# An already tuned two-block kernel whose build orders instructions by its other account of time

## The chip, the cores and the metric

The kernel runs on one core of a Trainium2 chip. The metric is the device time of one execution in microseconds, as the median of several runs. The engines are TensorE (PE in the profile, with PEld its weight loads), VectorE (DVE), ScalarE (ACT), GpSimd (POOL) and the queue that issues most DMAs (SP).

## What is computed

One sequence of 256 tokens with 1024 channels goes through two blocks, all in float32. The first has two layers; each layer is a half-weighted SwiGLU FFN, a mixer stage that feeds three sequence mixers from one projection, and another half FFN. The second block is an attention and convolution mixer modulated by a vector c, and a convolved SwiGLU FFN. The reference, cut:

```python
for l in range(2):
    x = x + 0.5 * swiglu(rms_norm(x, ffn1_norm[l]), ffn1_w_gate_up[l], ffn1_w_down[l])
    u = rms_norm(x, mix_norm[l]) @ w_in[l]
    u_ssd, u_ml, u_rw = jnp.split(u, [D_SSD_IN, D_SSD_IN + D_MLSTM_IN], axis=-1)
    y = concatenate([ssd_mixer(u_ssd, ...), mlstm_mixer(u_ml, ...), rwkv7_mixer(u_rw, ...)])
    x = x + y @ w_out[l]
    x = x + 0.5 * swiglu(rms_norm(x, ffn2_norm[l]), ffn2_w_gate_up[l], ffn2_w_down[l])
x = rms_norm(x, final_norm)
mod = silu(c) @ w_ada + b_ada                     # six vectors: shift, scale, gate, twice
h = rms_norm(x, g_mix) * (1 + sc1) + sh1
q, k, v, u, c_gate, b_gate = split(h @ w_in_2)
conv = b_gate * causal_dwconv(c_gate * u, conv_w, conv_b)
x = x + gt1 * (concat([rms_norm(attention(q, k, v)), rms_norm(conv)]) @ w_out_2)
h = rms_norm(x, g_ffn) * (1 + sc2) + sh2
val, gte = split(causal_dwconv(h @ w_up, ...))
out = rms_norm(x + gt2 * ((silu(gte) * val) @ w_down), g_final)
```

## The kernel before

Activations lie channels-first: a tile is 128 channels by 256 tokens. All weights come in as one stream of 128x128 blocks, seven to a chunk, in the order in which the program asks for them: `fetch` issues the DMA of a chunk (`raw`, L145), ScalarE casts it to a high part (`whi`, L155), VectorE makes the rest (`wlo`, L156). A dense product takes three matmuls for each block, high by high, high by low and low by high (`mm`, L172 to L176; in the profile L92, output `d`, of which there are three PSUM banks). The small float32 matmuls and transposes of the mixers are recorded at L95, output `m`, with four banks, when they belong to a chain that `weave` runs.

The mixer stage (`mixers`, L406) is where different kinds of work mix. The projection w_in is 40 column tiles, computed two at a time in the order of `IN_PAIRS`; each pair (`d_...`) takes 48 matmuls or more, and its results go through ScalarE and VectorE (`conv_silu` L394 to L401, `shifted` L426 to L430, the gates' input `dtg` L457, `sz` L476). Five generators run beside it: rwkv in two halves of four heads, the gates, the SSD heads and the mLSTM heads. `weave` (L508) decides in which order the program emits pairs of w_in, steps of the generators and tiles of w_out.

The steps that matter below, of one rwkv half: the kk norm (L569 to L597, matmuls `m_2814` and `m_2831` in the first layer's first half); the triangular inversion in two levels, for which four copies L699 each assemble `Tm` and `TT` (`w2_3296` and `w2_3297` for half 0, `w2_3948` and `w2_3949` for half 1), L719 and L723 take the products from PSUM, L732 and L733 subtract; then four chunks of state steps, each a ring from TensorE over a copy `R` (L756), a matmul, `uv` (L761), a matmul and the state `S` on VectorE (L771, L774), with the result copied by L780. The gates' block is one chain on ScalarE and VectorE (L824 to L837) with three loads of activation tables. The SSD heads fetch rows of the gates from DRAM (L1066), and ScalarE turns each into decays: four L1078 and one L1079 for each tile.

The program's order is a wish, not the queue. The tile framework collects all instructions, and its list scheduler then writes one in-order queue for each engine from dependencies, from priorities (`tc.high_priority`, in `first` and around the weight casts) and from an account of when each engine would be free. Semaphores are placed afterwards; the pools' buffers and PSUM banks rotate as written.

## Time and profile before

| | |
|---|---|
| median of 3 runs | 1607.62 us (1605.43 to 1609.72) |
| profiled execution | 1615.12 us, span 1613.3 us |
| mean granted TensorE clock in it | 0.986 of full |
| busy share: TensorE, its weight loads, VectorE, ScalarE | 97%, 94%, 72%, 61% |
| weights read | 287.5 MB, 179 GB/s over the span |

All stage times below are those of the one profiled execution: FFN 1 of layer 0 until about 208 us, its mixers until 485, FFN 2 until 668, FFN 1 of layer 1 until 850, its mixers until 1122, FFN 2 until 1300, the attention stage until 1415, the last FFN until 1613. Busy TensorE time counts from an instruction's start to its end while matmuls overlap, so what a dense matmul costs is read from how far apart their starts lie.

### The profile page before, as it was taken

The numbers are of one execution on the slowest core, as the hardware profiler recorded it, in microseconds if no ns is written. First come the engines' busy times: TensorE is split into PE (matmuls) and PEld (weight loads), VectorE is DVE, ScalarE is ACT, GpSimd is POOL, SyncE is SP. The second block draws the span as 40 slices with busy tenths as digits, with TensorE's granted clock in tenths as the row PEclk, the third lists the DMA queues.
The fourth block names the chain that finished last, engine by engine and source line by source line (L and its number), as shares of the span: only waits on it lengthen the run. The fifth ranks groups of instructions, "written<-read, shape, count | busy, mean of one in ns | idle before, by whom it ended". The sixth has DMA issues, their size and how long they took to land.

```text
span 1613.3 us, 33769 instructions
## 1 busy us (share of the span) xinstructions
PE 1561.7 (97%) x13660; PEld 1509.1 (94%) x13660; DVE 1161.1 (72%) x1965; ACT 990.7 (61%) x1684; POOL 44.6 (3%) x66
## 2 busy tenths in 40 slices
PE   8999998999999999999999999999999999999998
PEld 7999988879999999999998887899999998999997
DVE  7765689757777655787568975778785676698863
ACT  6554587878655444555457777866555565587753
POOL 0000001000000000000000100000000000000000
PEclk9999999899999999999999989999999999999999
DMA  7866644334357666597664333446886653456662
GB/s 255 296 205 190 200 127 127 96 117 140 115 174 258 222 184 194 185 336 253 192 197 134 119 100 113 140 126 202 296 310 189 190 159 115 149 163 189 188 193 73
DMA packets 106717, 290.81 MB, mean 180 GB/s; under 512 B 15640, under 2 KB 28096, under 8 KB 106432
## 3 DMA queue, kind: packets, MB, share of 16 engines
q1 hardware_dynamic: 106272, 288.12, 56.4%
q8 instruction: 107, 1.75, 0.5%
q10 hardware_dynamic: 288, 0.52, 0.1%
q14 instruction: 50, 0.41, 0.1%
HBM read 287.51 MB, written 1.09 MB: 179 GB/s over the span
## 4 chain that ended last, share of the span: by engine, by line
PE 71%; issue 16%; DVE 6%; ACT 5%; POOL 1%; DMA 0%; DVEq 0%; POOLq 0%; SPq 0%; ACTq 0%
PE d L92 60%; PE m L95 8%; PE m L92 3%; DVE wlo L156 1%; ACT whi L155 1%; PE st L92 1%; POOL stm L233 1%; ACT w L699 1%; DVE am L628 0%; DVE pair L227 0%; DVE tmp L338 0%; DVE w L399 0%; DVE pair L399 0%; ACT w L426 0%; DMA x<-xT 0%
## 5 line engine op out<-in xcount | busy, mean ns | idle before, releaser
L92 PE MATMUL d<-pair,whi 128*128 128x256 f32 x5344 | 960.3, 282 | 4.8 <-ACT whi L155 2.2
L92 PEld LDWEIGHTS d<-pair,whi 128*128 128x128 f32 x5344 | 824.3, 190 | 17.0 <-issue 6.3
L156 DVE TENSOR_TENSOR wlo<-raw,whi 128x896 fp32r<-128x896 f32 x544 | 590.9, 1089 | 250.5 <-ACT whi L155 247.2
L92 PE MATMUL d<-pair,wlo 128*128 128x256 f32 x2672 | 755.7, 283 | 3.9 <-DVE wlo L156 3.9
L155 ACT CAST whi<-raw 128x896 fp32r<-128x896 f32 x544 | 511.3, 943 | 329.0 <-PE d L92 232.8
L92 PEld LDWEIGHTS d<-pair,wlo 128*128 128x128 f32 x2672 | 509.2, 191 | 9.2 <-DVE wlo L156 5.2
L92 PE MATMUL d<-hp,whi 128*128 128x256 f32 x1760 | 302.7, 277 | 0.0
L92 PEld LDWEIGHTS d<-hp,whi 128*128 128x128 f32 x1760 | 265.9, 188 | 0.0
L92 PE MATMUL d<-hp,wlo 128*128 128x256 f32 x880 | 243.4, 277 | 0.0
L92 PEld LDWEIGHTS d<-hp,wlo 128*128 128x128 f32 x880 | 165.5, 188 | 0.0
L226 ACT CAST hp<-h 128x256 fp32r<-128x256 f32 x88 | 35.4, 406 | 93.3 <-DVE h L366 93.2
L95 PE MATMUL m<-w,w 64*64 64x64 f32 (+5 forms) x848 | 66.9, 260 | 8.1 <-issue 4.3
L95 PEld LDWEIGHTS m<-w,w 64*64 64x64 f32 (+3 forms) x848 | 55.6, 155 | 15.3 <-issue 11.9
L1146 DVE SCALAR_TENSOR_TENSOR adasum<-ada,sc,adasum 128x1024 f32<-128x1024 f32 x42 | 53.8, 1281 | 17.6 <-DMA ada<-ada 17.6
L227 DVE TENSOR_TENSOR hp<-h,hp 128x256 fp32r<-128x256 f32 x88 | 36.8, 422 | 15.3 <-ACT hp L226 14.5
L92 PE MATMUL d<-w,whi 128*128 128x256 f32 x256 | 45.6, 281 | 0.0
L1179 DVE SCALAR_TENSOR_TENSOR up<-raw,par,up 128x255 f32<-128x255 f32 (+1 forms) x88 | 37.2, 479 | 10.6 <-ACT raw L1175 10.4
L365 ACT ACTIVATE s<-d 128x256 f32<-128x256 f32 x80 | 30.4, 380 | 22.7 <-PE d L92 21.8
L95 PE MATMUL m<-cst,w 128*128 128x128 f32 (+1 forms) x166 | 29.6, 297 | 11.0 <-DVE w L989 4.1
L95 PE MATMUL m<-w,am 64*64 64x64 f32 (+1 forms) x512 | 33.7, 230 | 6.7 <-issue 6.7
L95 PEld LDWEIGHTS m<-w,am 64*64 64x64 f32 (+1 forms) x512 | 27.4, 140 | 13.4 <-issue 9.2
L92 PEld LDWEIGHTS d<-w,whi 128*128 128x128 f32 x256 | 39.1, 189 | 0.0
(341 smaller groups left out, 1481.2 us busy)
## 6 DMA issues: line engine op xcount, KB each, us to landing
raw<-ws SPq DMA_DIRECT2D x544, 448.0 KB, 3.9
ada<-ada SPq DMA_DIRECT2D x48, 512.0 KB, 6.4
w<-da SPq DMA_DIRECT2D x16, 256.0 KB, 4.9
w<-small SPq DMA_DIRECT2D x10, 256.0 KB, 4.4
ab<-abias SPq DMA_DIRECT2D x1, 1536.0 KB, 7.9
x<-xT SPq DMA_DIRECT2D x4, 256.0 KB, 5.5
w<-da SPq DMA_DIRECT2D x8, 128.0 KB, 3.4
w<-dw SPq DMA_DIRECT2D x4, 256.0 KB, 5.0
```

The costliest lines, as they stand in the source:

```text
L92: return op(*args, **kw)
L95: return op(*args, **kw)
L155: S.copy(hi, raw)
L156: V.tensor_sub(lo, raw, hi.bitcast(F32))
L226: S.copy(hi, src)
L227: V.tensor_sub(lo, src, hi.bitcast(F32))
L233: G.tensor_tensor(dst, m, mhalf.to_broadcast([128, n]), op=OP.pow)
L365: S.activation(s, p[:, 0], AF.Silu)
L699: S.copy(dst[g, :, o:o + 32].rearrange("p s (b c) -> p s b c", b=2), et[g, :, :, 0:8].rearrange("p c b s -> p s b c"))
L1146: V.scalar_tensor_tensor(acc, w, sc[:, k:k + 1], acc, op0=OP.mult, op1=OP.add)
L1179: V.scalar_tensor_tensor(dst[:, i, d:], raw[:, i, :T - d], P(w, 3 * j + k), dst[:, i, d:], op0=OP.mult, op1=OP.add)
```

## The change

The context that holds the list scheduler gets one argument. With it the scheduler takes its other account of time, a timeline for each engine, when it decides which ready instruction comes next. No instruction is added or taken away, the weight stream keeps its order, and GpSimd's queue is the same; the queues of TensorE, VectorE, ScalarE and SP are written in other orders.

```diff
     order = []
-    with tile.TileContext(nc) as tc:
+    with tile.TileContext(nc, schedule_with_timeline_sim=True) as tc:
         _program(tc, aps, order)
     r = run_bass_kernel_spmd(nc, [_pack(inp, order)], core_ids=[0])
```

Three places in the mixers of layer 0; layer 1 repeats each.

ScalarE around the first half's inversion. Names: `w2_3296` and `w2_3297` are Tm and TT, `w2_3531` the gates' input, `w2_3565` and `w2_3566` the gates' block. Before:

```order
L699 COPY w2_3296<-w2_3043 32x8x32 x4
L695 ACTIVATE w2_3042<-w2_3044,cst_71 128x16x16 x2
L719 ACTIVATE w2_3428<-m_3430,cst_71 128x8x16 x2
L699 COPY w2_3297<-w2_3043 32x8x32 x4
L457 ACTIVATE w2_3531<-d_3494,par_70 128x256
L155 CAST whi_3761<-raw_3626 128x896
L824 ACTIVATE w2_3565<-w2_3531 64x256
L394 ACTIVATE pair1_3252<-d_3721,par_70 128x256
L825 ACT_TABLE_LOAD
L825 ACTIVATE w2_3565<-w2_3565 64x256
```

Now:

```order
L824 ACTIVATE w2_3565<-w2_3531 64x256
L825 ACT_TABLE_LOAD
L825 ACTIVATE w2_3565<-w2_3565 64x256
L155 CAST whi_3870<-raw_3738 128x896
L827 ACT_TABLE_LOAD
L827 ACTIVATE w2_3566<-w2_3565 64x256
L395 COPY w2_3637<-d_3576 128x512
L695 ACTIVATE w2_3042<-w2_3044,cst_71 128x16x16 x2
L830 ACT_TABLE_LOAD
L830 ACTIVATE w2_3565<-w2_3566 64x256
L155 CAST whi_3897<-raw_3765 128x896
L699 COPY w2_3296<-w2_3043 32x8x32 x4
```

The gates' block with its three table loads stood behind both groups of L699; now the whole of it stands ahead of the first group, and a fourth load (L401) stands ahead of the second. Ahead of these rows now come two L394 that read d_3721. On TensorE `m_3430`, which reads Tm, stood behind 31 matmuls of d_3721; now it stands behind all 48 of d_3863 and 18 of d_4019, and 30 more of d_4019 follow it.

TensorE at the second half's inversion and its first state steps (`m_4280` second level, `m_4306`, `m_4313`, `m_4416`, `m_4433` the steps of chunks 0 and 1; `m_4398` to `m_4400` the first half's output; `m_4442` the SSD heads). Before:

```order
L95 MATMUL m_4280<-w2_3949,w2_4186 64x64
L95 MATMUL m_4306<-w2_3682,am_3395 64x64 x2
L92 MATMUL d_4471<-pair0_2490,whi_4251 128x256 x2
L92 MATMUL d_4471<-pair0_2490,wlo_4252 128x256
L92 MATMUL d_4471<-pair0_2490,whi_4345 128x256 x2
L92 MATMUL d_4471<-pair0_2490,wlo_4346 128x256
```

Now:

```order
L95 MATMUL m_4280<-w2_3949,w2_4186 64x64
L95 MATMUL m_4306<-w2_3682,am_3395 64x64
L95 MATMUL m_4280<-w2_3949,w2_4186 64x64
L95 MATMUL m_4306<-w2_3682,am_3395 64x64 x2
L95 MATMUL m_4313<-R_4311,w2_3949 64x64 x4
L95 MATMUL m_4306<-w2_3682,am_3395 64x64 x4
L95 MATMUL m_4398<-cst_71,w2_3706 128x128
L95 MATMUL m_4399<-cst_71,w2_3162 128x128
```

Before, ten matmuls of d_4471 stood between these rows of m_4306 and m_4313, and more between the later steps; now the steps follow each other. From m_4280 to m_4919, the last SSD group, there were 158 dense matmuls and are now 48, all of d_5014. The dense tiles d_4471 to d_4856 stand ahead of m_4188, the first matmul group of that level. Earlier in the stage, 15 dense matmuls stood between m_2814 and m_2831 and 46 do now.

ScalarE from the copy `R_4311`, which m_4313 reads, to L780, which empties the bank of m_4306 (`w2_4321` to `w2_4326` are the SSD heads' decays). Before, from that copy on:

```order
L756 COPY R_4311<-m_4306 64x256
L155 CAST whi_4502<-raw_4376 128x896
L761 ACTIVATE w2_3682<-m_4313 64x256
L1078 ACTIVATE w2_4321<-w2_4321,nat_3842 128x128 x4
L1078 ACTIVATE w2_4322<-w2_4322,nat_3842 128x128
L1079 ACTIVATE w2_4321<-w2_4321 128x512
L806 ACTIVATE w2_4411<-m_4398,par_70 128x256
L780 COPY w2_4305<-m_4306 64x256
L1078 ACTIVATE w2_4322<-w2_4322,nat_3842 128x128
L806 ACTIVATE w2_4411<-m_4398,par_70 128x256
L1078 ACTIVATE w2_4322<-w2_4322,nat_3842 128x128 x2
L155 CAST whi_4529<-raw_4479 128x896
```

Now, from the row behind that copy on:

```order
L1078 ACTIVATE w2_4321<-w2_4321,nat_3842 128x128 x4
L1078 ACTIVATE w2_4322<-w2_4322,nat_3842 128x128
L761 ACTIVATE w2_3682<-m_4313 64x256
L1078 ACTIVATE w2_4322<-w2_4322,nat_3842 128x128 x3
L1079 ACT_TABLE_LOAD
L1079 ACTIVATE w2_4321<-w2_4321 128x512
L1078 ACTIVATE w2_4325<-w2_4325,nat_3842 128x128 x4
L1078 ACTIVATE w2_4326<-w2_4326,nat_3842 128x128 x4
L1079 ACTIVATE w2_4322<-w2_4322 128x512
L1079 ACTIVATE w2_4325<-w2_4325 128x512
L806 ACTIVATE w2_4411<-m_4398,par_70 128x256
L780 COPY w2_4305<-m_4306 64x256
```

Between the copy and L780 stood five L1078 and one L1079; now 16 L1078, a table load and three L1079 do.

## Rows read from the trace of the kernel before

**Rows 1.** The page, busy time: engine, us busy, share of the span.
```profile
PE 1561.7 (97%) x13660; PEld 1509.1 (94%) x13660; DVE 1161.1 (72%) x1965; ACT 990.7 (61%) x1684; POOL 44.6 (3%) x66
```

**Rows 2.** Chain of work that ended last: start us, us, what.
```profile
30.49 93.91 PE d L92 x826
```

**Rows 3.** Windows: us, busy PE, PEld, DVE, ACT, POOL, clock, DMA share, GB/s.
```profile
208.00:485.00 277.00, 260.70 (x2396) 242.93 (x2394) 214.13 (x433) 202.96 (x372) 16.89 (x21) 0.97 0.42 128
485.00:668.00 183.00, 182.49 (x1577) 181.87 (x1578) 119.09 (x159) 93.08 (x139) 0.82 (x2) 1.00 0.66 208
```

**Rows 4.** Timeline, TensorE: start us, us, what, [idle before <- releaser].
```profile
226.43 1.05 PE L95 MATMUL m<-cst,w 128*128 128x2 f32 x8 [1.15 <-ACT w L575]
...
230.11 0.66 PE L95 MATMUL m<-cst,w 128*128 128x128 f32 x4 [0.75 <-ACT w L586]
...
240.29 1.16 PE L95 MATMUL m<-w,w 64*128 64x128 f32 x16 [0.71 <-DVE w L617]
...
252.86 1.33 PE L95 MATMUL m<-cst,w 128*128 128x2 f32 x10 [1.06 <-ACT w L575]
```

**Rows 5.** Timeline, TensorE, at cluster A.
```profile
275.56 0.38 PE L92 MATMUL d<-pair,wlo 128*128 128x256 f32 x1 [1.15 <-DVE wlo L156]
...
282.00 1.15 PE L95 MATMUL m<-w,am 64*64 64x64 f32 x32 [1.85 <-issue]
...
295.84 1.03 PE L95 MATMUL m<-w,w 64*64 64x64 f32 x28 [2.17 <-issue]
```

**Rows 6.** Timeline, ScalarE, the gates' block.
```profile
286.42 0.47 ACT L457 ACTIVATE w<-d,par 128x256 f32<-128x256 f32 x1
286.79 0.93 ACT L155 CAST whi<-raw 128x896 fp32r<-128x896 f32 x1
...
287.94 0.55 ACT L394 ACTIVATE pair<-d,par 128x256 f32<-128x256 f32 x1
288.51 1.28 ACT L825 ACT_TABLE_LOAD   x1
289.80 0.42 ACT L825 ACTIVATE w<-w 64x256 f32<-64x256 f32 x1
...
294.18 0.42 ACT L830 ACTIVATE w<-w 64x256 f32<-64x256 f32 x1
```

**Rows 7.** Timeline, TensorE, at cluster B.
```profile
336.43 0.76 PE L95 MATMUL m<-w,am 64*64 64x64 f32 x19 [1.50 <-issue]
...
340.55 0.65 PE L95 MATMUL m<-w,w 64*64 64x64 f32 x15 [0.73 <-ACT w L719]
...
354.89 0.30 PE L95 MATMUL m<-cst,w 128*128 128x128 f32 x1 [0.52 <-DVE w L794]
```

**Rows 8.** Windows over one stretch: all instructions, then those of L95 alone.
```profile
349.60:393.09 43.49, 42.97 (x407) 38.07 (x406) 28.72 (x53) 34.84 (x77) 1.64 (x1) 1.00 0.40 122
...
349.60:393.09 43.49, 23.84 (x248) 19.23 (x248) 1.00 0.40 122
```

**Rows 9.** Groups by line, ScalarE, 208 to 485: busy us, mean ns, idle before.
```profile
L1078 ACT ACTIVATE w<-w,nat 128x128 f32<-128x128 f32 x32 | 10.3, 392 | 0.0
L699 ACT COPY w<-w 32x256 f32<-32x256 f32 x16 | 10.2, 636 | 0.1
...
L1079 ACT ACTIVATE w<-w 128x512 f32<-128x512 f32 x8 | 4.9, 622 | 0.0
...
L780 ACT COPY w<-m 64x256 f32<-64x256 f32 x8 | 2.9, 365 | 4.4 <-PE m L95 4.4
```

**Rows 10.** Windows as in rows 3, of two short stretches.
```profile
283.70:287.10 3.40, 3.40 (x25) 3.17 (x25) 2.75 (x7) 3.34 (x7) 0.00 (x0) 0.50 0.78 217
297.30:307.60 10.30, 10.30 (x55) 8.81 (x54) 5.46 (x14) 5.65 (x12) 0.53 (x1) 0.50 0.16 46
```

**Rows 11.** Timeline, TensorE, end of the mixers.
```profile
405.78 0.43 PE L95 MATMUL st<-cst,stm 128*128 128x128 f32 x2 [0.57 <-POOL stm L233]
...
433.76 1.01 PE L95 MATMUL m<-cst,w 128*128 128x128 f32 x4 [1.91 <-DVE w L989]
```

## The prediction

> **What bounds the kernel now.** I read the page's busy times first: TensorE is busy for 97% of the span [rows 1], so whatever another order gives or takes must come out of TensorE's idle time and of how fast it runs. Next I read the chain of work that ended last: its long pieces are dense matmuls of one kind, 826 in 93.91 us, 113.7 ns each [rows 2]. That is the price of a dense matmul as cover: ten of them hide 1.1 us. The table of windows by stage then says where idle time is at all. An FFN stage has 182.49 us of TensorE work in 183 us; a mixer stage has 260.70 in 277 [rows 3] (the mixers of layer 1 read 257.62 in 272, the same pattern). So the mixers are the place: 16 us of idle in each, and beside it some 10 us in which TensorE runs at the half clock level. TensorE's timeline over the mixers gives the waits one by one. They fall into four clusters: early, where the first rwkv half starts [rows 4]; cluster A, its triangular inversion [rows 5]; cluster B, the second half's inversion and state steps [rows 7]; and the end [rows 11].
>
> **The change part by part.** No instruction is added or removed, so every term is a wait that moves. All cover is dense w_in matmuls: 16 tiles' worth, used up sooner or later.
>
> *Early: a gain.* Before, waits of 1.15, 0.75, 0.71 and 1.06 us, 3.67 in sum [rows 4]. Now more dense work stands ahead of each: between the kk norm's two steps m_2814 and m_2831 46 dense matmuls instead of 15, 31 × 0.1137 = 3.5 us more cover than the 0.75 us wait needs. I leave 0.3 us: **−3.4 us** per mixers. If the cover came too late for all of them the gain would be 0.
>
> *Cluster A: a loss.* Before, TensorE waits 1.15 + 1.85 + 2.17 = 5.17 us [rows 5]. In the old order the copies L699, which level 0 of the inversion needs, run ahead of the gates' block on ScalarE (L457 to L830 with its three table loads). In the new order that block stands ahead of them. From before's trace the block lasts from 286.42 to 294.60, 8.2 us [rows 6]; in the new order it holds two L695 (128x256 like L394) in place of two L394. Count from the end of d_3721, which the first row L394 ×2 reads:
> ScalarE: two L394 1.0, the block 8.2, a weight cast 0.93, four L699 2.5 (0.636 each [rows 9]), less 0.1 at each of three joins (neighbours overlap by about that: L155 starts at 286.79, before L457's 0.47 us from 286.42 are over): 12.3 us until m_3430 may start. TensorE meanwhile: d_3863 needs the bank that L457 empties, a wait of 1.6 us; then 48 + 18 dense matmuls, 7.5 us. So m_3430 waits 12.3 − 9.1 = 3.2 us. Then ScalarE has two L695 (1.2, each as an L1079), a cast (0.93), two L394 (1.0), a fourth table load (1.28 [rows 6]) with its L401 (0.62, as an L1079), four L699 (2.5) and two L719 (0.6, smaller than an L780 each), less overlaps 7.5 us, against m_3430 and 30 dense matmuls, 1.15 + 3.4 = 4.6 us: 2.9 us. Sum 7.7 against 5.17: **+2.5 us** per mixers. If the casts and L695 run in gaps it is 0; I keep +5 as the upper end.
>
> The sum takes a table load at 1.28 us with nothing around it: L825's load starts at 288.51 and its activation at 289.80 [rows 6]. The Trainium skill, page "ScalarE: Activation LUTs", section "What ACT_TABLE_LOAD costs", counts about 1.38 us of drain on top of each load, 2.66 us a switch. No such drain shows in that row; by that rule the four loads in this chain would add an estimated 5.5 us per mixers, 11 us in all, and the time would come to about 1632 us.
>
> *Cluster B: the main loss.* In the stretch 349.60 to 393.09 TensorE is idle for 0.5 us only, because 158 dense matmuls stand between the rwkv steps; the L95 matmuls are 248 of its 407 records [rows 8]. In the new order 48 remain there (d_5014): 110 × 0.1137 = 12.5 us of cover was spent earlier. TensorE's own work left is 43.0 − 12.5 = 30.5 us, and ScalarE's in-order queue between L723 and the last L1079 (68 instructions and three loads, at the means of [rows 6, 9] by shape 35.1 us, less 0.1 per join) 29 us: two queues of equal length that hand work back and forth, so each handover now shows. The largest, from the end of the copy R_4311: m_4313 waits for that copy (0.5 us: 0.37 [rows 9] and the two handovers); the next m_4306 waits for L761 behind five L1078 (five in 1.6 us, and 0.38: 1.5 us after TensorE is ready); and m_4416, which takes the bank that L780 empties, waits until ScalarE has done 16 L1078 (6.27), a table load (1.28), three L1079 (1.87), L761 (0.38, shaped as L780), one L806 (0.55, as an L394 [rows 6]) and L780, 10.7 us less 22 joins of 0.1 = 8.5 us, while TensorE, from 2.0 on, has 20 matmul records ahead of it at 0.1 us (24.9 us of L95 work over 248 in [rows 8]) and the fill of two short groups, until about 4.5: 4.0 us. Sum so far 6.0. Behind it stand the state copy and the steps m_4433, m_4465, m_4550, later m_4587, m_4692, m_4711 and m_4919 with nothing or one short group between them; at half a us each seven such steps make 3.5 us, of which I take 3 as some overlap. Together 9 us, against 1.50 + 0.73 + 0.52 = 2.75 before [rows 7]: **+6.2 us** per mixers. Bounds: with all handovers hidden −2.75, with every step at 0.7 us and the bank wait repeated once +11.
>
> *End and stage starts: nothing.* Before, 0.57 and 1.91 us at the end [rows 11]. Now w_out starts before the last rwkv group and waits for it; I put that at the same 2.5 us, from 0 to 5. At the other stage starts waits of 0.5 to 1.5 us come and go in both directions (a tile's h is made ahead of part of the activations' low half in some, behind it in others): 0, from −4 to +4 in all.
>
> *The clock.* TensorE's granted clock is 0.50, the 1.2 GHz level, from 283.70 to 287.10 and from 297.30 to 307.60 [rows 10]; ahead of them lie the waits that end at 282.00 and 295.84 [rows 5]. Cluster B's new waits are longer than those, so I count one more such stretch of 10.3 us per mixers. If dense work filled it, half its length, 5 us, would be lost; about 40% of it is dense or back to back work: **+2 us** per mixers (0 to 5).
>
> **Sum.** Per mixers −3.4 + 2.5 + 6.2 + 2 = +7.3, two layers +14.6, rounded to +14: against the profiled execution's 1615.1 us that is 1629, and against the median, 7.5 us below that execution, **1621 us**.
>
> **Rivals.**
> *Faster, the handovers stay hidden.* ScalarE's exponentials L1078/L1079 need only the gates and a load, no rwkv result. If ScalarE reaches them while TensorE still works off dense tiles, cluster B costs its floor, −2.75. Then a mixers costs −3.4 + 2.5 − 2.75 and no clock term, −3.7; with −2 at stage starts 1598 us. For it: ScalarE is busy only 202.96 of 277 us [rows 3], so it has slack to run ahead. Against: L723 behind m_4188 stands ahead of all those L1078 in its queue, and the dense tiles are used up before m_4188. It decides once cluster B's waits fall below 3.6 us.
> *No change.* Waits only change place: A +2.5, B +1, early −3.4, so 1607 us within 0.3% (5 us, about what a measurement of this kernel can tell from no change). For it: ScalarE and TensorE have the same work in B. Against: the 4.0 us bank wait alone exceeds that.
> *Much slower, the tail at half clock.* If TensorE is held at 1.2 GHz through the whole tail of each mixers, its 30.5 us of work there grows by up to 15; as part of that lies under waits, +10: per mixers +15, 1638 us. For it: 10.3 us at 0.50 followed two waits of 1.85 and 2.17 us [rows 5, 10]. Against: the 48 dense matmuls of d_5014 lie in between.
>
> **How the numbers follow.** My forecast, slower by 5 to 22 us, gets 0.48; much slower 0.12; the drain rule 0.03; no change 0.15; faster 0.22. Slower is then 0.63. The range 1597 to 1641 reaches to the faster rival's time and to the much slower one's; the forecast's own range is 1612 to 1631.
>
> **What would show it.** Right: early waits at L575 and L586 gone; in both mixers waits before m_3430 and at level 0's second group of 2 to 4 us, released by L699 and L719; a stretch some 30 us long near the end of w_in in which L95 rows follow each other with waits on L756, L761, L774 and L780, 8 us or more in sum. FFN stages as long as before within 2 us. Wrong: a mixers not longer than 277 us; the tail's L1078 done before m_4306; or a difference that sits in the FFN stages, say by weight casts that come late.

## The result, and the profile after

The changed kernel takes **1665.38 us** (median of 4 runs, 1663.71 to 1667.92) where the kernel before took 1606.71 beside it: 1.0355 times as long, 95% interval 1.0334 to 1.0376. The forecast was 1621, the range ended at 1641. The direction was right; the size was a quarter of what came (+14 forecast, +58.7 measured). The profiled executions lie 52.8 us apart, since that of the kernel before was some 8 us above its median.

The page of the changed kernel, busy times: TensorE's work is what it was, its share is not.

```profile
PE 1573.8 (94%) x13660; PEld 1525.2 (92%) x13660; DVE 1161.9 (70%) x1965; ACT 989.1 (59%) x1684; POOL 45.0 (3%) x66
```

Against [rows 1] the busy time grew by 12 us and the span by 52.8, so 40.7 us are new idle time of TensorE. The next two views are windows by stage, columns as in rows 3, with the stages cut at TensorE's last matmul of a named tile (`d_2517`, `d_5823`, `d_8136`, `d_10499`, `d_13809`, `d_16048`, `d_17279`), so that both kernels are cut at the same work. The order of the rows is FFN 1, mixers, FFN 2 of layer 0, the same of layer 1, attention, last FFN. Before:

```profile
0.00:209.30 209.30, 202.65 (x1714) 198.11 (x1715) 139.70 (x203) 111.21 (x170) 3.03 (x12) 1.00 0.70 225
209.30:479.10 269.80, 254.52 (x2344) 236.94 (x2343) 208.42 (x425) 199.12 (x366) 16.89 (x21) 0.97 0.43 128
479.10:666.40 187.30, 185.78 (x1607) 184.96 (x1606) 121.90 (x164) 95.48 (x143) 0.82 (x2) 1.00 0.66 207
666.40:851.10 184.70, 183.62 (x1616) 182.10 (x1615) 130.21 (x180) 95.61 (x144) 1.06 (x4) 1.00 0.72 236
851.10:1119.70 268.60, 254.22 (x2343) 236.71 (x2343) 208.39 (x426) 198.81 (x367) 16.93 (x21) 0.97 0.44 135
1119.70:1291.10 171.40, 171.22 (x1510) 169.81 (x1510) 122.52 (x161) 91.01 (x139) 0.00 (x0) 1.00 0.73 239
1291.10:1409.60 118.50, 114.90 (x899) 107.71 (x898) 80.74 (x156) 68.59 (x136) 4.24 (x4) 0.97 0.45 140
1409.60:1613.30 203.70, 194.76 (x1644) 192.74 (x1642) 149.24 (x255) 130.88 (x224) 1.60 (x2) 0.99 0.53 162
```

After:

```profile
0.00:212.20 212.20, 205.49 (x1715) 201.65 (x1715) 136.99 (x197) 110.45 (x168) 2.06 (x12) 0.99 0.69 224
212.20:492.60 280.40, 253.20 (x2342) 237.06 (x2341) 208.99 (x421) 197.76 (x364) 18.02 (x21) 0.95 0.40 122
492.60:683.60 191.00, 187.02 (x1608) 185.98 (x1606) 122.12 (x168) 96.25 (x144) 0.82 (x2) 0.99 0.64 205
683.60:871.30 187.70, 185.97 (x1616) 184.35 (x1615) 129.99 (x179) 95.99 (x145) 0.88 (x4) 1.00 0.70 234
871.30:1155.50 284.20, 255.65 (x2342) 239.91 (x2341) 209.08 (x422) 197.85 (x365) 18.63 (x21) 0.95 0.40 125
1155.50:1334.10 178.60, 174.62 (x1512) 173.10 (x1511) 125.04 (x170) 93.02 (x143) 0.00 (x0) 0.99 0.70 230
1334.10:1460.90 126.80, 117.67 (x899) 109.96 (x898) 80.66 (x157) 69.35 (x137) 3.20 (x4) 0.92 0.42 130
1460.90:1666.10 205.20, 194.14 (x1644) 193.16 (x1642) 149.00 (x255) 128.42 (x222) 1.39 (x2) 0.98 0.53 161
```

Length less busy TensorE is a stage's idle time. The two mixers are 10.6 and 15.6 us longer, and their idle time grew by 11.9 and 14.2. The six other stages, for which the forecast had nothing, are 26.6 us longer: 14.6 of it is idle time, and 12.0 is the same work running longer beside a lower granted clock (attention from 0.97 to 0.92; the clock's missing share times the length, summed over the six stages, grew from 5.6 to 20.1 us).

Where in the mixers: windows of layer 0 cut at the first matmul of `m_2814`, `m_3430` and `m_4188`. The last row is the tail. Before:

```profile
209.30:226.40 17.10, 15.93 (x134) 14.96 (x132) 13.20 (x21) 15.23 (x25) 0.00 (x0) 1.00 0.52 152
226.40:282.00 55.60, 49.20 (x438) 46.50 (x439) 52.04 (x119) 40.60 (x69) 7.74 (x10) 1.00 0.39 121
282.00:346.40 64.40, 59.76 (x638) 53.92 (x638) 45.05 (x106) 51.87 (x88) 2.42 (x5) 0.89 0.39 113
346.40:479.10 132.70, 129.63 (x1136) 121.57 (x1135) 98.13 (x182) 91.41 (x185) 6.74 (x6) 0.99 0.44 136
```

After:

```profile
212.20:229.30 17.10, 16.90 (x144) 16.19 (x143) 15.03 (x26) 15.88 (x27) 0.00 (x0) 1.00 0.43 136
229.30:295.60 66.30, 58.14 (x513) 55.67 (x511) 63.25 (x147) 50.59 (x84) 8.87 (x10) 1.00 0.42 133
295.60:364.30 68.70, 65.47 (x732) 60.77 (x732) 44.10 (x88) 49.62 (x83) 2.41 (x5) 0.98 0.42 123
364.30:492.60 128.30, 112.69 (x957) 104.43 (x956) 86.60 (x164) 81.67 (x172) 6.74 (x6) 0.91 0.38 113
```

Idle time changed by -1.0, +1.8, -1.4 and, in the tail, +12.5 us (layer 1, cut alike: -1.1, +3.4, +0.3 and +11.5). So the tail makes the loss. Its waits, from TensorE's timeline after:

```profile
369.83 0.35 PE L95 MATMUL m<-R,w 64*64 64x64 f32 x3 [2.10 <-DVE lst L790]
...
374.12 1.11 PE L95 MATMUL m<-w,am 128*64 128x64 f32 x8 [3.65 <-ACT w L761]
...
381.29 0.87 PE L95 MATMUL m<-w,w 128*128 128x128 f32 x4 [2.66 <-ACT w L780]
...
406.28 0.68 PE L95 MATMUL m<-S,w 128*128 128x128 f32 x4 [0.91 <-DVE S L774]
...
420.28 0.50 PE L92 MATMUL d<-w,whi 128*128 128x256 f32 x2 [1.60 <-ACT w L395]
...
426.27 2.93 PE L95 MATMUL m<-w,w 128*128 128x256 f32 x16 [1.06 <-ACT w L401]
```

With seven smaller ones that are left out here, ten waits in cluster B make 12.4 us and three at the end 3.2, where [rows 7, 11] had 2.75 and 2.5. (One more, 1.70 us at 338.19 behind L761, stands ahead of `m_4188` and is not among the ten.) ScalarE's timeline beside the second wait shows why it is 3.65:

```profile
372.10 1.57 ACT L1078 ACTIVATE w<-w,nat 128x128 f32<-128x128 f32 x5 [2.73 <-DMA w<-da]
373.69 0.38 ACT L761 ACTIVATE w<-m 64x256 f32<-64x256 f32 x1
```

L761, which `m_4306` waits for, stands behind five L1078, as the forecast had it; but those five first wait 2.73 us themselves, for rows of the gates from DRAM (L1066). Layer 1 does not repeat this place: there L761 stands ahead of the L1078 in ScalarE's queue (1034.01 against 1035.89), and the waits of its counterparts of `m_4313`, `m_4306` and `m_4416` read:

```profile
1033.04 0.65 PE L95 MATMUL m<-R,w 64*64 64x64 f32 x8 [0.72 <-DVE w L733]
1034.44 0.68 PE L95 MATMUL m<-w,am 128*64 128x64 f32 x8 [0.76 <-ACT w L761]
...
1044.54 1.22 PE L95 MATMUL m<-w,w 128*128 128x128 f32 x4 [4.16 <-ACT w L780]
```

The start of an FFN, which the forecast passed over: TensorE at FFN 2 of layer 0, the last statistics matmul and the next two waits.

```profile
492.59 0.38 PE L92 MATMUL st<-cst,stm 128*128 128x128 f32 x2
495.92 0.38 PE L92 MATMUL d<-pair,whi 128*128 128x256 f32 x1 [2.95 <-ACT pair L226]
497.32 0.39 PE L92 MATMUL d<-pair,whi 128*128 128x256 f32 x1 [1.02 <-DVE pair L227]
```

The first tiles of an FFN (`d_5822`, `d_5823`) read activations that are not normalized yet and need no statistics; the next (`d_5968`) wait for `rb`, L226 and L227. Before, 54 matmuls of `d_5822` and `d_5823` stood behind the statistics matmul and ran while that chain ended, 54 x 0.1137 = 6.1 us of cover; now none does, all stand ahead of it. Before, that place read:

```profile
472.71 0.38 PE L92 MATMUL st<-cst,stm 128*128 128x128 f32 x2
472.85 0.48 PE L92 MATMUL d<-pair,whi 128*128 128x256 f32 x2
```

### The profile page after: what moved, and what is told of

Read it like the earlier page. It is cut to its first block, busy times and chain, and to the rows that moved or that the text cites. A ratio compares the mean times of both kernels' runs of the same rounds, so it can differ in the third digit from the quotient of the medians.

```text
span 1666.1 us, 33832 instructions
## 1 busy us (share of the span) xinstructions
PE 1573.8 (94%) x13660; PEld 1525.2 (92%) x13660; DVE 1161.9 (70%) x1965; ACT 989.1 (59%) x1684; POOL 45.0 (3%) x66
## 4 chain that ended last, share of the span: by engine, by line
PE 60%; issue 12%; DVE 5%; ACT 5%; DMA 1%; POOL 0%; POOLq 0%; DVEq 0%; SPq 0%; ACTq 0%
PE d L92 51%; PE m L95 6%; PE m L92 3%; DVE wlo L156 1%; DMA w<-da 1%; ACT w L1078 1%; PE st L92 1%; ACT whi L155 1%; DVE tmp L338 0%; ACT w L699 0%; ACT L401 0%; DVE am L628 0%; DVE w L641 0%; ACT w L1079 0%; ACT L1079 0%
## 5 line engine op out<-in xcount | busy, mean ns | idle before, releaser
L155 ACT CAST whi<-raw 128x896 fp32r<-128x896 f32 x544 | 512.3, 944 | 447.0 <-PE d L92 307.8
L92 PE MATMUL d<-hp,whi 128*128 128x256 f32 x1760 | 306.1, 279 | 0.1
L95 PE MATMUL m<-w,w 64*64 64x64 f32 (+5 forms) x848 | 74.2, 275 | 15.4 <-ACT w L780 6.8
L95 PEld LDWEIGHTS m<-w,w 64*64 64x64 f32 (+3 forms) x848 | 61.7, 164 | 25.7 <-ACT w L780 8.0
L226 ACT CAST hp<-h 128x256 fp32r<-128x256 f32 x88 | 35.0, 403 | 30.3 <-DVE h L366 30.2
L95 PE MATMUL m<-w,am 64*64 64x64 f32 (+1 forms) x512 | 34.2, 235 | 14.2 <-issue 7.7
L95 PEld LDWEIGHTS m<-w,am 64*64 64x64 f32 (+1 forms) x512 | 28.2, 145 | 20.7 <-issue 10.2
L366 DVE TENSOR_TENSOR h<-s,d 128x256 f32<-128x256 f32 x88 | 36.1, 415 | 5.2 <-ACT s L365 5.2
L227 DVE TENSOR_TENSOR hp<-h,hp 128x256 fp32r<-128x256 f32 x88 | 36.3, 418 | 1.9 <-ACT hp L226 1.9
```

Source lines behind the costliest of these rows:

```text
L92: return op(*args, **kw)
L95: return op(*args, **kw)
L155: S.copy(hi, raw)
L226: S.copy(hi, src)
L227: V.tensor_sub(lo, src, hi.bitcast(F32))
L366: V.tensor_mul(h, s, p[:, 1])
```

## The experiments

Two theories stood at first. Theory C, cover: the new account spends dense matmuls early, and the slow chains end with nothing beside them. Theory S, queue: the state loads L1066 stand behind weight chunks on SP, and ScalarE waits for them. Later runs set the orders of engines, not of single instructions, against each other. A kernel's stage times come from its one profiled execution.

**State loads on another queue (e1, e4).** In the changed kernel, and as a control in the one before:

```diff
-                    nc.sync.dma_start(t, da[q * 4:q * 4 + 4, c * 128:c * 128 + 128].unsqueeze(0)
+                    nc.gpsimd.dma_start(t, da[q * 4:q * 4 + 4, c * 128:c * 128 + 128].unsqueeze(0)
```

> The new order, with the SSD heads' loads of gate rows (L1066) issued by GpSimd instead of the SP queue. Theory C (cover: the dense matmuls now stand ahead of the chains, so every handover between TensorE and ScalarE lies open): the handovers stay, at most 6 us come back, 1659 to 1666 us. Theory S (queues: the chain's transfers and copies stand in in-order queues behind weight-stream instructions that wait): the 10.2 us that SP is held before these loads, and the landings of 5.55 and 5.75 us in the chain that ended last, go in both mixers, 16 to 25 us come back, 1640 to 1650 us.

> The kernel before with the SSD loads (L1066) issued by GpSimd, as a control for the first run. Both theories: before, these loads are issued 10 us ahead of their first use (343.25 against 353.32), nothing waits for them, so 1607 us within 0.3%; if issuing from GpSimd costs something by itself it shows here.

Measured: 1663.79 us in the changed kernel (ratio to before 1.035, 1.0302 to 1.0397), 1607.37 in the control (0.9992, 0.9974 to 1.0011). The 3.65 us wait fell to 0.47, but the next wait, which ended 5.8 us later, took 5.15 for a VectorE result (L794): the idle time of layer 0's tail was 17.1 us. Theory S falls. The wait removed there only uncovered the next one.

**Cover held back in the changed kernel (e2, e8).** A w_in tile may not pass chain matmuls that were traced more than two tiles earlier:

```diff
+                marks.append(PE.last)
+                if name and len(marks) > LAG:
+                    PE.pin = marks[-1 - LAG]
```

> The new account of time, but a w_in tile may not pass chain matmuls that the program wrote more than two tiles earlier: 539 dense matmuls stand between m_2814 and m_4280 (before 545, new order 706). Theory C: both mixers come back to about 272 us each, 1640 us (1633 to 1647); the stage starts and the attention stage stay slow. Theory S: ScalarE's and SP's queues are still written by the new account, so at most 8 us come back, 1657 us or more.

The same for four tiles only (`if name in ("z6", "xm2", "o0", "o2")`):

> The changed kernel, with four w_in tiles (z6, xm2, o0, o2) held on TensorE behind the chain matmuls traced two tiles earlier: 562 dense matmuls stand ahead of m_4188 instead of 706, so the last 144 are left for cluster B. Cover theory: cluster B's 12.4 us of waits fall to about 3, mixers 8 to 12 us shorter each, 1641 to 1650 us. ScalarE-order theory: the waits move to the places from which cover was taken, mixers within 3 us of the changed kernel's 280.4 and 284.1.

Measured: 1676.95 us (1.0438, 1.041 to 1.0467) and 1660.36 (1.0318, 1.0276 to 1.0361). With four tiles held the tail's idle time fell only to 13.0 us, and the segment ahead of it rose from 3.2 to 8.5; the mixers took 283.6 and 280.9. With every tile held they took 286.9 and 292.2. The gain that theory C promised did not come: in the changed kernel, cover given to the tail is missed ahead of it.

**Cover spent early in the kernel before (e3).** The first matmul of `m_4188` is put behind the dense tile o0, nothing else:

```diff
+                if name == "o0":
+                    behind(PE.late, PE.dense)
```

> The kernel before with its own account, but the first matmul of the second half's level 1 (m_4188) is put behind the dense tile o0, so that 716 dense matmuls stand ahead of it instead of 539, as in the new order (706). Theory C: this alone makes each mixers 10 to 15 us longer, 1627 to 1637 us. Theory S: SP and ScalarE keep the old account's queues, so under 5 us in all, 1605 to 1612 us.

Measured: 1628.42 us (1.0135, 1.0105 to 1.0166). The mixers took 281.7 and 284.0 us, as long as the changed kernel's 280.4 and 284.2; idle time rose by 9.3 and 8.8. These lengths are those of the slowest of five executions (1638.01), at a clock of 0.95 and 0.93. So early cover by itself makes a large part of the mixers' loss, not shown to be all: 18.1 of the changed kernel's 26.1 us of new idle time, and 19.8 us of time (1628.42 against 1608.62 beside it). Of layer 0's 9.3 us, 5.9 arose in the tail, where the changed kernel has 12.5. The edit also makes `m_4188` itself later (162.9 us into the stage, 152.1 in the changed kernel), and the held tiles (e8) say that cover is not all that the changed kernel does to the mixers.

**ScalarE's gates block (e5, e6).** Its first activation held behind the first half's last L699 in the changed kernel:

```diff
-        S.activation(e0[w, 0], dg[w], AF.Abs)
+        behind(S.activation(e0[w, 0], dg[w], AF.Abs), b["l699", 0])
```

> The changed kernel, with the gates' first activation (L824) held on ScalarE behind the first half's last L699 copy, so that the copies which level 0 of the inversion needs come ahead of the gates' block again, as before. ScalarE-order theory: the waits in cluster A (6.4 us in the changed kernel, layer 0) fall to about 3, mixers 3 to 5 us shorter each, 1656 to 1660 us in all. Cover theory (what counts is how many dense matmuls are left for the tail): the wait only turns up later, mixers within 2 us of the changed kernel's 280.4 and 284.1, 1662 to 1669 us.

The reverse in the kernel before, the first L699 behind the block's last exponential (`behind(b["l699", 0][0], gate)`):

> The kernel before, with the first half's L699 copies held on ScalarE behind the gates' last exponential (L830): the changed kernel's order of those two blocks alone. The prediction's term for cluster A was +2.5 us per mixers, so 1612 us (1610 to 1615), with a longer wait ahead of the first matmul of the inversion. Cover theory: dense tiles in reach fill it, 1606 to 1609 us.

Measured: 1683.81 us (1.0473, 1.043 to 1.0517) and 1607.45 (0.9986, 0.9965 to 1.0007). In the changed kernel the wait ahead of `m_3430` fell from 3.54 to 2.42, and the one at the level's second group rose from 1.39 to 5.83. In the kernel before, the order that the forecast charged with +2.5 us costs no time that can be told; in its profiled execution the mixers have 0.8 and 4.6 us more idle time, but a higher granted clock (0.98 and 1.00 for 0.97).

**Weight casts behind the statistics (e7).** At an FFN's start ScalarE's casts L155 are held behind the copy L273 in the changed kernel:

```diff
-            S.copy(hi, raw)
+            cast = S.copy(hi, raw)
+            if hold:
+                behind(cast, hold[0])
```

> The changed kernel, with each FFN stage's (and the last FFN's) weight casts L155 held on ScalarE behind the copy L273 that ends the stage's row statistics, so that no cast that waits for TensorE stands ahead of the statistics. If such casts cause the longer stage starts: 2 to 4 us back at each of ffn2_0, ffn2_1, ffn1_0 and ffn_2, 1653 to 1659 us in all. If the starts are late for another reason (DVE's order, the late end of the mixers): within 2 us of the changed kernel's 1665, or worse where casts then come late.

Measured: 1678.17 us (1.0424, 1.0379 to 1.0469). Idle time of the FFN stages behind the mixers fell from 4.0 to 2.7 and 1.3, but new waits came for the held casts (1.30 us on `whi` at 494.55), and the mixers took 286.0 and 286.1. Undoing one pair of ScalarE's rows did not give the time back.

**Whole engines pinned (e9 to e13).** A table holds the order of before for an engine, and each instruction of the changed kernel is put behind its predecessor in it (order alone, no wait); what isn't pinned the scheduler orders by the new account. First TensorE alone, then with ScalarE, with VectorE, and those two without TensorE:

```diff
+    made = {i.name: i for i in nc.cur_bb.bb.instructions}
+    for runs in ORDERS.values():
...
+                    if prev is not None:
+                        tc.add_manual_dep(i, prev.name, mybir.DependencyInfo(mybir.DependencyClass.NoSync, mybir.DependencyReason.DATA), reason="order")
+                    prev = i
```

> The changed kernel's scheduler, but TensorE's whole order is pinned to that of the kernel before (each instruction behind its predecessor there); the scheduler orders ScalarE, VectorE and the queues around it by its new account. TensorE-order theory: 1607 to 1618 us, mixers within 3 us of 269.8 and 268.6. Theory that the other engines' orders cost it: 1640 us or more, the waits on ScalarE or VectorE stand in the mixers and at the stage starts.

> As the pin of TensorE's order, with ScalarE's whole order pinned to that of before as well; VectorE and the queues are free. ScalarE-order theory: 1605 to 1612 us while the pin of TensorE alone stays well above. VectorE theory: no better than the pin of TensorE alone. TensorE-order theory: both near 1610 us.

> As the pin of TensorE's order, with VectorE's whole order pinned to that of before as well; ScalarE and the queues are free. VectorE theory: 1605 to 1612 us while the pin of TensorE alone stays well above. ScalarE theory: no better than the pin of TensorE alone. TensorE-order theory: both near 1610 us.

> The changed kernel's scheduler with ScalarE's and VectorE's orders pinned to those of before and TensorE free (about 40% of its reordering against before remains). TensorE-order theory: still 1635 us or more. Theory of the other engines: 1605 to 1615 us.

> The changed kernel's scheduler with TensorE's, ScalarE's and VectorE's orders all pinned to those of before; only the DMA queue on SyncE is left to the new account. If the loss lies in the three engines' orders: 1604 to 1612 us, no change against before. If the queue's order has a share: above 1615 us.

| pinned to before | us | ratio, 95% | mixers, us | FFN 2, idle us | attention, us |
|---|---|---|---|---|---|
| nothing (the change) | 1665.38 | 1.0334 to 1.0376 | 280.4, 284.2 | 4.0, 4.0 | 126.8 |
| TensorE | 1708.13 | 1.0588 to 1.0645 | 313.3, 311.3 | 0.0, 0.0 | 123.2 |
| TensorE, ScalarE | 1654.58 | 1.0244 to 1.0303 | 287.0, 281.7 | 0.0, 0.0 | 117.0 |
| TensorE, VectorE | 1666.61 | 1.0305 to 1.0374 | 292.0, 292.0 | 1.5, 0.2 | 122.1 |
| ScalarE, VectorE | 1690.27 | 1.0475 to 1.0522 | 292.9, 289.5 | 3.7, 2.4 | 133.6 |
| all three | 1606.02 | 0.9967 to 1.001 | 270.8, 268.3 | 1.2, 0.2 | 114.7 |
| (kernel before) | 1606.71 | | 269.8, 268.6 | 1.5, 0.2 | 118.5 |

No single-engine theory holds for the mixers. With all three pinned the loss is gone, so SP's new order costs nothing by itself, and neither do the pins. With any one of the three left free a mixers stage is 13 to 23 us longer than before (43 with two left free), in five of six cases longer than in the changed kernel, where all three follow the new account: an order costs by how it meets the other engines' orders. FFN and attention are another matter. FFN 2 has no more idle time than before wherever TensorE's order is pinned, and more where it is free. Attention comes back where ScalarE is pinned beside TensorE; windows of the attention stage, TensorE and ScalarE pinned, then TensorE and VectorE:

```profile
1318.10:1435.10 117.00, 112.74 (x898) 105.54 (x897) 80.64 (x156) 68.03 (x135) 3.61 (x4) 0.99 0.43 141
```

```profile
1337.40:1459.50 122.10, 113.23 (x899) 105.55 (x898) 80.02 (x156) 68.63 (x135) 4.24 (x4) 0.99 0.42 135
```

Idle time is 4.3 against 8.9 us (3.6 before, 9.1 after). Which of ScalarE's rows it is was not tried. The last FFN, though, is 217.5 us long with TensorE and ScalarE pinned (203.7 before), so there too orders that do not belong together cost time.

**By stage (e14, e15, e18).** All engines and SP pinned, but only what is traced inside the mixers, then only what is outside them, then TensorE alone outside them:

```diff
+        n = len(nc.cur_bb.bb.instructions)
         acc, xg = mixers(l, acc, xg)
+        inside.update(i.name for i in nc.cur_bb.bb.instructions[n:])
...
+                if i is not None and (i.name in inside) is MIXERS:
```

> The changed kernel's scheduler with what is traced inside the two mixers stages pinned, on all engines and the queue, to the order of before; the other stages are left to the new account. If the loss belongs to each stage's own orders: the mixers back within 3 us of 269.8 and 268.6, the others as in the changed kernel, 1635 to 1642 us. If it is one of mismatched engines at the seams: 1655 us or more.

> The reverse: everything outside the mixers pinned to the order of before, the mixers left to the new account. Separable by stage: the mixers within 3 us of 280.4 and 284.1, the FFN and attention stages back to before, 1632 to 1640 us. Otherwise 1655 us or more.

> The changed kernel's scheduler with TensorE's order alone pinned to that of before outside the mixers; ScalarE, VectorE, the queue and the mixers are left to the new account. If the late FFN starts are dense matmuls used up ahead of the statistics: idle time in the two FFN stages behind the mixers falls from 4.0 us each to 1.5 or less, 1655 to 1660 us in all; attention stays at 9 to 12 us of idle time, if ScalarE's order is its cause. If the starts are late by ScalarE's or VectorE's orders: idle time there stays at 3 us or more, 1662 to 1669 us.

Measured: 1635.03 us (1.0169, 1.0131 to 1.0208), 1647.72 (1.0238, 1.0179 to 1.0296) and 1660.95 (1.0319, 1.0289 to 1.0349). The loss separates by stage, within the spread: the new order outside the mixers costs 25.5 us by itself, inside them 38.2, in sum 63.7 against 58.7 for both. With the mixers pinned they were back at 271.0 and 268.9; with the rest pinned every other stage was back. But e15 hit neither of its ranges, and its executions took 1637 to 1657 us: its mixers were 289.1 and 288.0 long, not 280.4 and 284.2, mostly by a clock of 0.92 and 0.94 instead of 0.95 (idle time 28.2 and 31.0 against 27.2 and 28.6). With TensorE alone pinned outside the mixers, FFN 2 of layer 0 has no idle time left:

```profile
502.00:683.90 181.90, 181.90 (x1606) 181.27 (x1606) 120.22 (x165) 95.61 (x142) 0.82 (x2) 1.00 0.67 213
...
1156.10:1327.50 171.40, 171.10 (x1510) 169.78 (x1510) 121.77 (x163) 91.32 (x139) 0.00 (x0) 1.00 0.73 241
```

These are that stage and the one of layer 1. Together they are 16.3 us shorter than in the changed kernel (7.7 of it idle time), though the time fell by 4.4 only: the mixers, whose orders were free, came out 291.6 and 286.3 long, at a clock of 0.92 and 0.94. So the late FFN starts are TensorE's order; that it is the dense matmuls used up ahead of the statistics fits the rows, and no run put only these back. Attention stayed at 128.1.

**Inside the mixers (e17, e16).** The pins on mixers instructions traced from `m_4188` on, then on those ahead of it (`int(i.name[2:]) < CUT[l]`):

> The changed kernel's scheduler with only the tail of each mixers stage (what is traced from m_4188 on) pinned to the order of before on all engines, so that 539 dense matmuls stand ahead of m_4188 as before; the first part of the mixers and the other stages are left to the new account. If the mixers' loss is made in the tail by want of cover: mixers within 4 us of 269.8 and 268.6, 1635 to 1645 us. If it is made ahead of the tail, by the orders there: mixers at 278 to 290, 1660 us or more.

> The changed kernel's scheduler with only the first part of each mixers stage (what is traced ahead of m_4188) pinned to the order of before on all engines; the tail is left to the new account, which then has 649 dense matmuls ahead of m_4188 instead of 706 (539 before) and 67 instead of none between m_4188 and m_4416. If the loss is the cover missing in the tail: idle time ahead of m_4188 as before (about 12 us from the stage's start), 8 to 12 us in the tail, mixers 273 to 278 us, 1647 to 1657 us in all. If the first part's orders make it: tail below 5 us, mixers at 272 or less, 1635 to 1645 us.

Measured: 1656.82 us (1.0305, 1.0259 to 1.035), mixers 282.1 and 276.8; 1666.32 (1.0348, 1.0311 to 1.0385), mixers 282.8 and 282.5. Windows from `m_3430` to `m_4188` and of the tail, with the tail pinned, then with the first part pinned:

```profile
299.30:364.80 65.50, 53.72 (x555) 47.30 (x555) 35.41 (x79) 41.84 (x74) 2.48 (x5) 0.79 0.31 89
364.80:497.60 132.80, 129.14 (x1132) 121.36 (x1131) 94.71 (x172) 89.17 (x181) 6.73 (x6) 0.99 0.41 130
```

```profile
282.40:363.10 80.70, 73.35 (x748) 67.42 (x748) 50.83 (x111) 58.49 (x95) 2.42 (x5) 0.89 0.38 111
363.10:492.00 128.90, 117.17 (x1022) 108.95 (x1021) 89.86 (x167) 85.12 (x176) 7.34 (x6) 0.96 0.41 126
```

With the tail pinned its idle time is 3.7 us, near the 3.1 of before, but 11.8 stand in the segment ahead of it, where 4.6 stood, at a clock of 0.79 instead of 0.89. `m_4188` starts 149.3 us into the stage behind as many dense matmuls as before, where these took 137.1. So the first part's new order has its chains ready some 12 us later (6 in layer 1), 8.0 of it idle time, and in the changed kernel 706 dense matmuls from `m_2814` to `m_4188` instead of 539, 167 x 0.1137 = 19.0 us more, hide that. With the first part pinned the chains are early again, but the new account still puts 649 dense matmuls there, and the tail lacks them (11.7 us). Neither run hit a range: the pinned tail fell between its two, the pinned first part above both. In new idle time of both mixers together it is 16.5 us with the tail pinned and 20.4 with the first part pinned, in sum 36.9; with neither pinned it is 26.1. The halves cost less together than by themselves, as they would if both draw on the same dense matmuls, which can stand in one place only. In the time, pinning the first part returned nothing and pinning the tail 8.6 us.

## Why the prediction was wrong

*Where it failed.* The step "End and stage starts: nothing" is the one that failed: "a tile's h is made ahead of part of the activations' low half in some, behind it in others" looked at the wrong rows. Outside the mixers 26.6 us arose in the trace, and with the mixers pinned (e14) 25.5 remained. The FFN starts in it are the very mechanism that the forecast used in the mixers, dense cover spent ahead of a chain (54 matmuls behind the statistics, now none), which the rows show and e18 ties to TensorE's order. Attention, +8.3, gained 5.5 us of idle time and lost clock; it hangs on ScalarE's order beside TensorE's (e10 against e11), and the single row stays open. For the mixers the forecast had +14.6; they came out 26.2 longer in the trace, and by e15 their share of the time is 38.2 us.

*Cluster B* had the right place and mechanism and too small a size: +6.2 forecast, +9.6 measured in the waits of layer 0 (12.4 against 2.75). Its three single prices, 0.5, 1.5 and 4.0 us for `m_4313`, `m_4306` and `m_4416`, fit layer 1 (0.72, 0.76 and 4.16), though L761 stands ahead of the L1078 there; in layer 0 they came as 2.10, 3.65 and 2.66. The forecast had taken the rows that ScalarE's exponentials read as landed, which explains the 3.65. The 2.10 is another matter: `m_4313` also reads what VectorE's subtraction L733 writes, and L733 ended only at 369.69, behind the first half's L789. (The 24.9 us of L95 work that the forecast cites read 23.84 in [rows 8]; its 0.1 us a record stands.) The end, forecast unchanged at 2.5, came as 3.2.

*Early* was forecast at -3.4 and came as about -0.6: the waits at L586 and the first at L575 are gone, but of the second at L575 0.64 is left, and 1.14 and 1.25 us stand in other places. *Cluster A* was put at 7.7 us of waits and came as these 6.4:

```profile
284.06 0.50 PE L92 MATMUL d<-pair,whi 128*128 128x256 f32 x2 [1.47 <-ACT w L457]
...
295.63 1.39 PE L95 MATMUL m<-w,am 64*64 64x64 f32 x32 [3.54 <-issue]
...
303.40 1.81 PE L95 MATMUL m<-w,w 64*64 64x64 f32 x55 [1.39 <-issue]
```

The walk along ScalarE's rows was right (1.6, 3.2 and 2.9 forecast), but reading it as the price of those rows was not: e6 has the same swap in the old orders at no cost in time. The two terms' sum was -0.9; the three segments ahead of the tail changed by -0.6 in layer 0 and +2.6 in layer 1.

*The clock* is the other mis-sized term. The clock's missing share times the length grew by about 6 us in each mixers and by 14.5 outside them. In the mixers much of it lay under waits, as their length grew no more than their idle time; outside most of it shows, as 12.0 us of longer work. The stretch behind the bank wait, after, with the one ahead of it and the one at the start of FFN 2:

```profile
371.50:378.30 6.80, 4.18 (x20) 3.60 (x20) 1.39 (x2) 6.12 (x16) 0.00 (x0) 0.50 0.38 108
...
381.20:394.80 13.60, 11.91 (x66) 9.83 (x67) 7.00 (x18) 6.48 (x19) 0.00 (x0) 0.52 0.01 2
...
497.80:501.20 3.40, 3.40 (x19) 3.40 (x18) 2.85 (x9) 1.90 (x5) 0.00 (x0) 0.50 0.00 1
```

The second is the forecast's "one more such stretch", 13.6 us for 10.3, at 0.52, close to the 1.2 GHz level, right behind the waits of 3.65 and 2.66 us. The first was not forecast; it begins within the wait of 3.65 us. In cluster A, on the other hand, only 3.4 us at that level are left (296.4 to 299.8) of the 13.7 in [rows 10]. The third, behind the waits of 2.95 and 1.02 us, is clock lost outside the mixers.

*The rivals.* Faster and no change are refuted by the tail's 15.6 us. "Much slower, the tail at half clock" named 1638, and its mechanism was partial: the tail's mean clock is 0.91, not half. The drain rule has no share: in the changed kernel too a load is 1.28 us, begins 0.01 us after the activation ahead of it ends (L824, at 284.46) and is followed within 0.02 us by its own (284.47 and 285.77 for L825). That agrees with the load's length in the Trainium skill, page "ScalarE: Activation LUTs", section "What ACT_TABLE_LOAD costs", and not with the drain that it adds.

## What to carry to other kernels

When a scheduler's account changes, look at every place where a chain ends beside bulk work, in every stage, and count the bulk instructions that stand behind the chain's last step: here the same count gave the loss in the mixers' tails and at the FFN starts, and only one of the two had been counted. The waits that one engine's order shows could not be mended one by one here (e1, e5, e7); a stage's orders belong together, and pinning them by stage, all engines at once, was what told the shares apart. Bulk work is a budget: two faults that draw on it can cost less together than each by itself, so undoing one alone can return little or nothing.

## What was not expected of the hardware

Dense matmuls run at two paces at the same granted clock, in stretches that can last for 90 us and more (before, from 486 to 576 us and from 1426 to 1556). Windows over the same place of FFN 2, the kernel before and the kernel with all three engines pinned, whose TensorE order is the same:

```profile
505.00:560.00 55.00, 55.00 (x469) 55.00 (x469) 39.45 (x50) 27.04 (x42) 0.00 (x0) 1.00 0.78 257
```

```profile
505.00:560.00 55.00, 55.00 (x487) 55.00 (x487) 41.07 (x52) 27.80 (x43) 0.00 (x0) 1.00 0.80 271
```

That is 117.3 ns a matmul against 112.9 at a clock of 1.00 and no idle time. Counted over runs of ten dense matmuls in a row, the share at the longer pace was 0.35 in the profiled execution before, 0.40 after and 0.10 to 0.47 in the other profiles; before and with all three engines pinned, with the same order on TensorE, it was 0.35 and 0.20, so the order does not set it. At some 4.4 ns on the 9,200 dense matmuls counted, the difference between 0.10 and 0.47 is 15 us of an execution. Stages are therefore better compared by idle time than by length; the cause is open.
